# SSM input in scratch memory as it stands in its tile, and lag products with their sides exchanged, in a hybrid SSM and attention block

## The chip, the cores and the metric

The kernel runs on one NeuronCore of a Trainium2 chip. The metric is device time in microseconds (us); the time of a kernel is the median of its runs. Engines are named as in the profile: PE (TensorE), PEld (its weight loads), DVE (VectorE), ACT (ScalarE), POOL (GpSimd) and SP (SyncE, which issues most of the DMAs here). A q behind a name (SPq, POOLq) marks what an engine's sequencer issues.

## The reference

One layer over 2048 tokens of 1024 channels, in float32. In the core of it:

```
hn = rmsnorm(h, g_mix);  u, gate_ssm, q, k, v, gate_attn = split(hn @ w_in)     # 512 columns each
y_ssm = s5_branch(u, ...) * silu(gate_ssm)      # 32 groups of 16 channels, 64 complex states a group,
                                                # y = Re(C x) + D u, then GELU, then GLU
y_att = stick_breaking(q, k, v) * silu(gate_attn)                               # 8 heads of 64
h = h + concat(y_ssm, y_att) @ w_out
h = h + sigmoid(rmsnorm(h, g_ple) @ w_ple_gate) * (p @ w_ple_proj)
```

## The kernel before

The work has five stages. In the **u stage** (`phase_u`, `ssm_chain`) u = hn @ w_in[:, :512] is made for eight pairs of token tiles, T = 0 to 7, of 256 tokens each. In the **SSM stage** (`ssm_pack`, `ssm_batch`, `gate_unit`, the first `attn_proj`) eight batches of four groups go through the recurrence, while the gate of the SSM half and the first projections of attention are made. Then come the four passes of attention, into whose end the GLU is laid, and the two output products. Precise products are made of three float32r products (`mm3`): both sides are split into a high and a low part, the high one by ACT, the low one by DVE (`split`, L505).

**u stage.** For each T from 1 on, `load_x` loads two tiles x of 128 tokens, squares them with a sum on ACT (L599), makes the norm's factor r by a DVE operation (L498) and a power on POOL (L501), scales x by it on ACT (L604), transposes x on PE into `ps_x` (L605, the helper's line L520), splits the result into `xt` (L607, ACT L507 and DVE L66) and stores `xt` for later stages as `hn` (L608). T=0 is loaded transposed already (`load_plain`), and for T=0 and 1 (RAW = 2) the norm is not applied to x but to u, as a row `e.row[T]`, which `norms` makes (L577). Then 96 products of 256 columns a T fill four banks `ps_u` (L634, helper lines L535 to L537). ACT copies each bank to `uq` (L639), and for T < 2 POOL multiplies it by the row (L641). After T=3 and T=7 each of the four `uq` tiles, one for 128 channels, is stored by POOL (L644) to scratch `u` of shape [16, 128 channels, 128 chunks], in pieces of 64 values (256 B).

**The chain.** Beside it `ssm_chain` makes what depends on parameters alone: step sizes, exponentials and sines (small operations on DVE), powers of the decay for 16 steps (`cmul`, L221, on DVE), the factors fr and fis (L228 to L240), the scaled input matrices bb and bbs (L248 to L253, six operations of 128x512), and tables of rotations, whose products already lie on POOL (`cmul` with aside, L171 to L173), stored as `tb` (L300). `vt` (L65) is the helper for DVE operations of two operands; in a profile they carry its line, L66.

**SSM stage.** For each batch of four groups `ssm_pack` makes input matrices `bn` (DVE) and output matrices `stC` (POOL, L329 to L331), transposes `bn` on PE by fours into `ps_pack` (L337) and copies it to `stB` (ACT, L338). Then come the lag products (L343): eight float32 products with a 128x128 block of `bn` as the stationary side and 16 columns of `cts` as the moving side; their copy `lags` (L346) goes to memory, from which `raw` is loaded with shifts. `ssm_batch` loads `us` (L372), one transfer of 512 KB a batch in pieces of 2 KB, two buffers; it multiplies it by `stB` into `ps_b` (L391), rotates and scans on DVE, ACT and POOL, and after it makes the output in `ps_y` (L452 to L455), GELU and the store `z`. `gate_unit` makes 24 products for each of four `ps_sg` tiles a T (L659), in banks o and z0; ACT and DVE make the gate `sg`, stored as `gs` (L668).

**The order of the work.** The code does not fix it. A planner (`plan`, `list_schedule`, `best_order`, from L1304) knows a modelled duration of every instruction (`duration`, L1271) and schedules each engine's list greedily, by ranks that come from a pass backward in time, over six turns. Every engine, and each DMA queue, then runs its list in that order, and waits where an operand or a buffer is late. Hints bend the order: what stands under `e.first()` goes ahead of everything, a DMA under `e.later(T)` is not issued before the instruction behind `e.mark(T)` starts, what stands under `e.abreast()` stays together in its order. At T=2 (L626) the mark for the later weights is set: those of the gate and of the first attention pass, and late constants.

The diff and what calls it, with the line numbers that the profile uses:

Of the kernel before, what the change touches and what calls it, by code (L numbers as in the profile page):

```python
# [8 lines left out]
F32 = mybir.dt.float32  # L9
# [9 lines left out]
P = 128  # L19
# [32 lines left out]
RAW = 2  # L52
MARK0, MARK1 = 7, 6
# [122 lines left out]
def ssm_chain(e, keep, sm):  # L176
# [25 lines left out]
    bst, bsw, R.cts, R.ct2 = bs[:, 0], bs[:, 1], ct[:, 0], ct[:, 1]  # L202
    vs(nc, R.cts, R.cts, sgn, ALU.mult)
# [3 lines left out]
    vt(nc, x1, lr, dt, ALU.mult)  # L207
    small_exp(e, sm, mag, x1, G)
    vt(nc, th, li, dt, ALU.mult)
    small_sincos(e, sm, sn, cs, th, G)  # L210

# [92 lines left out]
def ssm_pack(e, sm, R, b):  # L304
# [29 lines left out]
    for q in range(GB * HS // 4):  # L334
        ps = e.bank("ps_pack", "w0", "w1")
        for k in range(4):
            nc.tensor.transpose(ps[:, k * P:(k + 1) * P], bnf[:, 4 * q + k], e.ident)  # L337
        nc.scalar.activation(mbf[:, 4 * q:4 * q + 4].rearrange("p g m -> p (g m)"), ps, AF.Copy)  # L338
    ps = e.bank("ps_pack", "w0", "w1")
    for s in range(HS):  # L340
        for k in range(GB):
            o = (s * GB + k) * GH
            nc.tensor.matmul(ps[:, o:o + GH], bnf[:, HS * k + s], R.cts[:, b * GB + k, :], start=True, stop=True)  # L343
# [17 lines left out]
def by_group(d, b):  # L361

    n = P // GH
    return d[b * GB // n].rearrange("(s j) (h g) c -> (j h) s (g c)", s=HS, h=GH)[:, :, b * GB % n * NCH:(b * GB % n + GB) * NCH]


def ssm_batch(e, pool, mb, mc, b):
# [4 lines left out]
    nc.sync.dma_start(us.rearrange("p s k c -> p s (k c)"), by_group(e.u_d, b))  # L372
# [167 lines left out]
def phase_u(e, pool, xp, chain):  # L540
# [50 lines left out]
    def load_x(T):  # L591
        xt = xp.tile([P, 2, 2, NC8, P], F32R, tag="xg", name="xt", bufs=2)
        for hf in range(2):
# [18 lines left out]
    with e.first():  # L612
        xts[0], w = load_plain(0)
        with e.later(0):
            xts[1] = load_x(1)
        norms()
    prep = chain()
    for T in range(NT // 2):
# [7 lines left out]
        if T == 2:  # L626
            e.mark(T)
# [8 lines left out]
        for ct in range(4):  # L636
            k0 = (T % 4) * n
            o, out = ps[ct].rearrange("p (c j) -> p j c", j=L), uq[ct][:, :, k0:k0 + n]
            nc.scalar.activation(out, o, AF.Copy)  # L639
            if T < RAW:  # L640
                nc.gpsimd.tensor_tensor(out, out, e.row[T].rearrange("p (c j) -> p j c", j=L), op=ALU.mult)  # L641
            if T % 4 == 3:
                c0 = (T // 4) * (NCH // 2)
                nc.gpsimd.dma_start(e.u_d[ct][:, :, c0:c0 + NCH // 2].rearrange("j p c -> p j c"), uq[ct])  # L644
# [3 lines left out]
def gate_unit(e, pool, w, T, xt):  # L648
# [6 lines left out]
    for ct in range(4):  # L655
        o = e.bank("ps_sg", "o", "z0")[:, :256]
# [382 lines left out]
def hybrid_block_kernel(ctx: ExitStack, tc: tile.TileContext, x, xt, small, p, w_in, ssm_w_glu, w_out, w_ple_gate,  # L1039
# [16 lines left out]
    e.u_d = [scratch(f"u{k}", [L, P, NCH]) for k in range(4)]  # L1056
# [82 lines left out]

    e.first, e.later, e.mark = (lambda: hint("first")), (lambda T=2: hint(T)), (lambda T: rows.append((len(nc.cur_bb.bb.instructions), T, "mark")))  # L1140
# [130 lines left out]
def duration(i, name, outs, ins, psum):  # L1271
# [5 lines left out]
    if name == "InstMatmult":  # L1277
# [6 lines left out]
        return (1 if half else 2) * max(cols / 1160.0, 0.056), 0.12  # L1284
# [220 lines left out]
def best_order(ops, pre, soft, length, mode, rows, turns=6):  # L1505

    first, last, inner, soon = set(), set(), set(), set()
    hints = [r for r in rows if len(r) == 3]
    mark = {T: a for a, T, kind in hints if kind == "mark"}
    for a, b, kind in hints:  # L1510
        for k in range(a, b):
            if kind == "first":
                soon.add(k)
            elif kind in mark and type(ops[k]).__name__ == "InstDMACopy":
# [14 lines left out]
    for _ in range(turns):  # L1529
        order, start, done = list_schedule(ops, pre, soft, length, mode, lead([k - 1e5 if k in soon else r for k, r in enumerate(rank)], first))  # L1530
# [67 lines left out]
```

## Time and profile before

| | |
|---|---|
| median of 3 runs | 1563.97 us (1562.64 to 1567.96) |
| the profiled execution | 1565.11 us, its span 1563.4 us |
| busy: PE, DVE, ACT, POOL | 1484.2, 1057.6, 931.2, 844.9 us |
| u stage (until the last copy of `ps_u`) | 0 to 131.6 us |
| SSM stage, roughly | 131.6 to 330 us |
| mean granted TensorE clock | 0.984 |

The profile shows one execution. Busy time is the time in which an engine had an instruction running; matmuls are pipelined, so that PE's busy time counts their overlap once, and the distance from one start to the next is what a product costs. An operation on a line is written as its output, an arrow and its inputs, by the names of the program's tiles. 128x512 f32 x16 means sixteen instructions on tiles of 128 partitions and 512 values. 64*128 after a PE instruction is the part of the array that it uses, rows by columns. A product of float32 operands appears as two instructions (passes). Text behind a group in brackets or bars says how long the engine had been idle before it, and who ended that.

### The profile page before, as it was taken

Reading aid. Unit: us, or ns where it says so; the run is one execution under the profiler, and the core shown is the slowest. Engines: PE = TensorE matmul, PEld = TensorE weight load, DVE = VectorE, ACT = ScalarE, POOL = GpSimd, SP = SyncE. Lnnn points to the kernel's source line nnn. Section 1 sums busy time; section 2 is a strip of 40 time slices with the busy share of each in tenths; the row PEclk is TensorE's granted clock in tenths of the full one; section 3 lists DMA queues with packets and bytes.
Section 4 is the critical chain, followed back from the end, with each engine's and each line's share of the span. In section 5 each row is a group of like instructions: output and inputs, shape, how many; then the busy total and the mean of one; then the engine's idle time right before and its main releaser. Section 6 shows DMA issues by size and latency. Waiting matters only on the chain.

```text
span 1563.4 us, 34915 instructions
## 1 busy us (share of the span) xinstructions
PE 1484.2 (95%) x13120; PEld 1261.9 (81%) x13120; DVE 1057.6 (68%) x1953; ACT 931.2 (60%) x2069; POOL 844.9 (54%) x1131
## 2 busy tenths in 40 slices
PE   8899999889999999998999988999999999999998
PEld 7899989878888888887888876777776888777776
DVE  7845868657677877678768785666869556754544
ACT  6553545456677877677867777666765435633432
POOL 3843433435556666565666598774565654433433
PEclk9999999999999999999999998999999999999999
DMA  8767636454332422334223365763347645622211
GB/s 334 273 248 216 205 109 208 147 182 157 139 110 95 134 94 95 108 116 136 91 89 116 127 222 167 234 181 95 104 147 252 200 162 182 196 68 93 89 61 61
DMA packets 168377, 236.22 MB, mean 151 GB/s; under 512 B 63504, under 2 KB 109712, under 8 KB 156816
## 3 DMA queue, kind: packets, MB, share of 16 engines
q1 hardware_dynamic: 166272, 226.50, 44.4%
q0 software_dynamic: 1936, 7.49, 1.7%
q8 instruction: 104, 1.70, 0.5%
q14 instruction: 65, 0.53, 0.1%
HBM read 169.05 MB, written 64.90 MB: 150 GB/s over the span
## 4 chain that ended last, share of the span: by engine, by line
PE 77%; DVE 8%; ACT 5%; issue 4%; POOL 3%; DMA 2%; POOLq 0%; SPq 0%; ACTq 0%; DVEq 0%
PE ps_q L744 20%; PE ps_o L848 6%; PE ps_z L809 6%; PE ps_wt L520 4%; PE ps_g L713 3%; PE ps_g L715 3%; PE ps_h L713 3%; PE ps_h L714 3%; PE ps_g L714 3%; PE ps_h L715 3%; DVE px L825 2%; DMA wst<-in_ssm_w_glu_dram 1%; PE ps_sg L535 1%; PE ps_u L535 1%; PE ps_u L536 1%
## 5 line engine op out<-in xcount | busy, mean ns | idle before, releaser
L827 POOL TENSOR_TENSOR be<-be,px 128x512 f32<-128x512 f32 (+3 forms) x320 | 317.3, 996 | 205.8 <-DVE px L825 157.2
L744 PE MATMUL ps_q<-w_w,xt 64*128 64x512 f32 x2880 | 406.1, 404 | 11.4 <-DVE v L66 9.7
L825 DVE TENSOR_TENSOR_SCAN px<-px,ps_z 128x512 f32<-128x512 f32 (+3 forms) x320 | 339.8, 1086 | 103.5 <-ACT be L819 73.8
L744 PEld LDWEIGHTS ps_q<-w_w,xt 64*128 64x128 f32 x2880 | 297.5, 187 | 52.8 <-issue 9.5
L814 ACT ACTIVATE px<-ps_z 128x512 f32<-128x512 f32 (+3 forms) x320 | 162.8, 540 | 76.9 <-PE ps_z L809 58.8
L840 ACT ACTIVATE ws<-ps_wt 128x512 f32<-128x512 f32 (+3 forms) x320 | 164.9, 550 | 62.7 <-PE ps_wt L520 62.4
L819 ACT ACTIVATE be<-ps_z 128x512 f32<-128x512 f32 (+3 forms) x320 | 167.8, 555 | 0.5 <-PE ps_wt L520 0.5
L809 PE MATMUL ps_z<-k,q 64*128 64x512 f32 (+3 forms) x960 | 148.9, 384 | 14.0 <-DVE px L825 11.1
L848 PE MATMUL ps_o<-ws,v 128*64 128x128 f32 x2176 | 140.1, 281 | 1.0 <-ACT ws L840 1.0
L848 PEld LDWEIGHTS ps_o<-ws,v 128*64 128x64 f32 x2176 | 120.3, 139 | 19.6 <-issue 15.6
L520 PEld LDWEIGHTS ps_wt<-ident,be 64*128 64x128 f32 x2176 | 104.5, 142 | 28.8 <-POOL be L827 8.9
L809 PEld LDWEIGHTS ps_z<-k,q 64*128 64x128 f32 x960 | 97.1, 189 | 33.3 <-DVE px L825 17.3
L520 PE MATMUL ps_wt<-ident,be 64*128 64x64 f32 x2176 | 111.5, 229 | 8.0 <-ACT ws L840 3.2
L1020 POOL TENSOR_TENSOR sg<-sg,h 128x512 f32<-128x512 f32 x32 | 44.8, 1411 | 114.3 <-DVE sg L66 114.3
L501 POOL TENSOR_TENSOR rs_qk<-rs_qk,mhalf 128x4 f32<-128x4 f32 x64 | 65.7, 1027 | 42.4 <-DVE rs_qk L73 41.6
L535 PE MATMUL ps_u<-xt,w_w 128*128 128x256 f32 x256 | 75.9, 297 | 6.6 <-ACT w_w L485 6.1
L536 PE MATMUL ps_u<-xt,w_w 128*128 128x256 f32 x256 | 75.4, 295 | 2.1 <-DVE xt L66 2.1
L66 DVE TENSOR_TENSOR yr<-sx,yr 128x512 fp32r<-128x512 f32 x64 | 53.4, 854 | 34.9 <-ACT yr L507 34.1
L823 POOL TENSOR_SCALAR_AFFINE_SELECT px<-px 128x128 f32<-128x128 f32 x128 | 39.4, 318 | 69.1 <-ACT px L814 67.5
L537 PE MATMUL ps_u<-xt,w_w 128*128 128x256 f32 x256 | 74.6, 294 | 0.0
L507 ACT ACTIVATE yr<-sx 128x512 fp32r<-128x512 f32 x64 | 39.3, 628 | 52.1 <-POOL sx L906 20.5
L1014 ACT ACTIVATE sg<-sg,rs 128x512 f32<-128x512 f32 x24 | 17.4, 725 | 74.0 <-DVE sg L66 74.0
(421 smaller groups left out, 3694.9 us busy)
## 6 DMA issues: line engine op xcount, KB each, us to landing
xt<-hn SPq DMA_DIRECT2D x60, 1024.0 KB, 4.9
hn<-xt SPq DMA_DIRECT2D x16, 1024.0 KB, 8.5
h<-h SPq DMA_DIRECT2D x64, 256.0 KB, 3.5
wst<-in_w_in_dram SPq DMA_DIRECT2D x48, 256.0 KB, 5.5
xg<-hn SPq DMA_DIRECT2D x12, 1024.0 KB, 7.0
out_dram<-sg SPq DMA_DIRECT2D x32, 256.0 KB, 2.5
x<-in_x_dram SPq DMA_DIRECT2D x14, 512.0 KB, 6.5
h<-in_x_dram SPq DMA_DIRECT2D x28, 256.0 KB, 4.4
```

Source lines behind the costliest of these rows:

```text
L520: e.nc.tensor.transpose(ps[h][:, 64 * k:64 * k + 64], v[r], e.ident[r, r])
L535: mm(out, wh, xh, start=first, stop=False)
L713: mm(out, xh, wh, start=first, stop=False, skip_group_check=more)
L714: mm(out, xh, wl, start=False, stop=False, skip_group_check=more)
L744: nc.tensor.matmul(o, xt[r, a, c], A.w[c][r, b], start=c + s == 0, stop=c == NC8 - 1 and s == 2)
L809: nc.tensor.matmul(z[:, :n], q[half[h], a], A.k[ch][half[h], b, :n], start=s == 0, stop=s == 2)
L814: nc.scalar.activation(px[:, :n], z[:, :n], AF.Sigmoid, scale=-(HD ** -0.5))
L819: nc.scalar.activation(be[:, :n], z[:, :n], AF.Sigmoid, scale=HD ** -0.5)
L825: nc.vector.tensor_tensor_scan(rv, rv, z[:, :n][:, ::-1], initial=1.0 if carry[h] is None else carry[h], op0=ALU.mult, op1=ALU.bypass)
L827: nc.gpsimd.tensor_tensor(be[:, :n], be[:, :n], px[:, 1:n + 1], op=ALU.mult)
L840: nc.scalar.activation(dst, ps, AF.Copy)
L848: nc.tensor.matmul(po[half[h], :P], A.v[sb][:, h], w[:, h, b], start=sb == i, stop=sb == 0)
```

## The change

The scratch `u` becomes eight arrays of [128 channels, 16, 64 chunks], one for each tile `uq`, so that a partition is stored as one piece of 4 KB, and SP issues the store instead of POOL. The load of `us` becomes sixteen transfers a batch of 32 KB each, in pieces of 64 values. The lag products exchange sides: four products a batch with 32 columns of `ct` as the stationary side and 256 columns of `bn` as the moving side, each on 32 columns of the array, put side by side in one bank; ACT copies them to `lt`, PE transposes that twice, and ACT copies the half that is wanted to `lags`.

With these come others. In `ssm_chain` the two-operand operations after the sines, and the power products, go from DVE to POOL. The row products of T=0 and 1 go from POOL to DVE; for T=1 DVE reads `ps_u` itself and ACT's copy is left out. `norms` is no longer under `e.first()`. The x transposes and their splits get a new hint, `ahead`, which lowers their rank by LEAD = 12 in the planner. The mark of the later weights goes from T=2 to T=4. `ps_pack` uses bank w0 alone, and `ps_sg` gets w1 as a third bank. The planner's duration of a float32 product on 32 columns or fewer becomes a quarter of that on the whole array.

```diff
+LEAD = 12
+LATER = 4
...
-    vt(nc, x1, lr, dt, ALU.mult)
+    nc.vector.tensor_tensor(x1, lr, dt, op=ALU.mult)
     small_exp(e, sm, mag, x1, G)
-    vt(nc, th, li, dt, ALU.mult)
+    nc.vector.tensor_tensor(th, li, dt, op=ALU.mult)
     small_sincos(e, sm, sn, cs, th, G)
+    def vt(nc, out, a, b, op):
+        nc.gpsimd.tensor_tensor(out, a, b, op=op)
...
-        cmul(e, sm, pr[:, n + 1:2 * n + 1], pi[:, n + 1:2 * n + 1], pr[:, 1:n + 1], pi[:, 1:n + 1], *bc, [n, G])
+        cmul(e, sm, pr[:, n + 1:2 * n + 1], pi[:, n + 1:2 * n + 1], pr[:, 1:n + 1], pi[:, 1:n + 1], *bc, [n, G], True)
...
     for q in range(GB * HS // 4):
-        ps = e.bank("ps_pack", "w0", "w1")
+        ps = e.bank("ps_pack", "w0")
...
-    ps = e.bank("ps_pack", "w0", "w1")
+    ps = e.bank("ps_pack", "w0")
+    flat = R.ct.rearrange("p k g h -> p (k g h)")
+    with e.abreast():
+        for k in range(GB):
+            o = (b * GB + k) * GH
+            nc.tensor.matmul(ps[2 * GH * k:2 * GH * (k + 1), :HS * P], flat[:, o:o + 2 * GH], bnf[:, HS * k:HS * (k + 1)].rearrange("p s m -> p (s m)"), start=True, stop=True)
+    lt = sm.tile([P, HS * P], F32, tag="lt", name="lt")
+    nc.scalar.activation(lt, ps[:, :HS * P], AF.Copy)
+    ps = e.bank("ps_pack", "w0")
     for s in range(HS):
-        for k in range(GB):
-            o = (s * GB + k) * GH
-            nc.tensor.matmul(ps[:, o:o + GH], bnf[:, HS * k + s], R.cts[:, b * GB + k, :], start=True, stop=True)
+        nc.tensor.transpose(ps[:, s * P:(s + 1) * P], lt[:, s * P:(s + 1) * P], e.ident)
...
-    nc.scalar.activation(lags[:, :HS], ps[:, :HS * GB * GH].rearrange("p (s g h) -> p s g h", s=HS, h=GH), AF.Copy)
+    nc.scalar.activation(lags[:, :HS], ps[:, :HS * P].rearrange("p (s g v h) -> p s g v h", s=HS, v=2, h=GH)[:, :, :, 0], AF.Copy)
...
-def by_group(d, b):
-    n = P // GH
-    return d[b * GB // n].rearrange("(s j) (h g) c -> (j h) s (g c)", s=HS, h=GH)[:, :, b * GB % n * NCH:(b * GB % n + GB) * NCH]
+def by_group(d, g, s):
+    return d.rearrange("(h g) (s j) c -> g s j h c", s=HS, h=GH)[g, s]
...
-    nc.sync.dma_start(us.rearrange("p s k c -> p s (k c)"), by_group(e.u_d, b))
+    half, n = NCH // 2, P // GH
+    for h in range(2):
+        for s in range(HS):
+            for k in range(GB):
+                g = b * GB + k
+                nc.sync.dma_start(us[:, s, k, h * half:(h + 1) * half], by_group(e.u_d[g // n][h], g % n, s))
...
-            for h, ps in enumerate(turned(e, "ps_x", ("tr", "ssm") if hf else ("z0", "z1"), [x[:, c * P:(c + 1) * P] for c in range(NC8)])):
-                d = slice(64 * h, 64 * h + 64)
-                split(e, xt[:, hf, 0, :, d], xt[:, hf, 1, :, d], ps)
+            with e.ahead():
+                for h, ps in enumerate(turned(e, "ps_x", ("tr", "ssm") if hf else ("z0", "z1"), [x[:, c * P:(c + 1) * P] for c in range(NC8)])):
+                    d = slice(64 * h, 64 * h + 64)
+                    split(e, xt[:, hf, 0, :, d], xt[:, hf, 1, :, d], ps)
...
     with e.first():
         xts[0], w = load_plain(0)
         with e.later(0):
             xts[1] = load_x(1)
-        norms()
+    norms()
...
-        if T == 2:
-            e.mark(T)
+        if T == LATER:
+            e.mark(2)
...
-            nc.scalar.activation(out, o, AF.Copy)
+            if T != 1:
+                nc.scalar.activation(out, o, AF.Copy)
             if T < RAW:
-                nc.gpsimd.tensor_tensor(out, out, e.row[T].rearrange("p (c j) -> p j c", j=L), op=ALU.mult)
+                vt(nc, out, o if T else out, e.row[T].rearrange("p (c j) -> p j c", j=L), ALU.mult)
             if T % 4 == 3:
-                c0 = (T // 4) * (NCH // 2)
-                nc.gpsimd.dma_start(e.u_d[ct][:, :, c0:c0 + NCH // 2].rearrange("j p c -> p j c"), uq[ct])
+                nc.sync.dma_start(e.u_d[ct][T // 4], uq[ct])
...
-        o = e.bank("ps_sg", "o", "z0")[:, :256]
+        o = e.bank("ps_sg", "o", "z0", "w1")[:, :256]
...
-    e.u_d = [scratch(f"u{k}", [L, P, NCH]) for k in range(4)]
+    e.u_d = [[scratch(f"u{k}{h}", [P, L, NCH // 2]) for h in range(2)] for k in range(4)]
...
-        return (1 if half else 2) * max(cols / 1160.0, 0.056), 0.12
+        return (0.5 if outs[0][0] <= 32 else 1 if half else 2) * max(cols / 1160.0, 0.056), 0.12
...
-        order, start, done = list_schedule(ops, pre, soft, length, mode, lead([k - 1e5 if k in soon else r for k, r in enumerate(rank)], first))
+        order, start, done = list_schedule(ops, pre, soft, length, mode, lead([k - 1e5 if k in soon else r - LEAD if k in ahead else r for k, r in enumerate(rank)], first))
```

More of the change, by code (lines that the diff above doesn't have):

```diff
@@ L202, in ssm_chain @@
     bst, bsw, R.cts, R.ct2 = bs[:, 0], bs[:, 1], ct[:, 0], ct[:, 1]
+    R.ct = ct
     vs(nc, R.cts, R.cts, sgn, ALU.mult)
@@ L1138, in hint @@
         rows.append((n, len(nc.cur_bb.bb.instructions), kind))
+    e.ahead = lambda: hint("ahead")
     e.first, e.later, e.mark = (lambda: hint("first")), (lambda T=2: hint(T)), (lambda T: rows.append((len(nc.cur_bb.bb.instructions), T, "mark")))
@@ L1505, in best_order @@
 def best_order(ops, pre, soft, length, mode, rows, turns=6):
-    first, last, inner, soon = set(), set(), set(), set()
+    first, last, inner, soon, ahead = set(), set(), set(), set(), set()
     hints = [r for r in rows if len(r) == 3]
@@ L1513, in best_order @@
                 soon.add(k)
+            elif kind == "ahead":
+                ahead.add(k)
             elif kind in mark and type(ops[k]).__name__ == "InstDMACopy":
```

## The prediction

> **What bounds the kernel now.** I read the page first, then the busy time by stage, then who waited for whom on PE, then the timeline around the longest waits. The page, and under it the u stage (0 to 131.6 us) and the SSM stage (to 330 us): after length and busy us of PE, weight loads, DVE, ACT and POOL, each row ends with PE's granted clock, DMA share and GB/s.
>
> ```profile
> span 1563.4 us, 34915 instructions
> PE 1484.2 (95%) x13120; PEld 1261.9 (81%) x13120; DVE 1057.6 (68%) x1953; ACT 931.2 (60%) x2069; POOL 844.9 (54%) x1131
> ...
> 0.00:131.60 131.60, 117.19 (x1049) 114.00 (x1050) 83.58 (x246) 69.74 (x128) 79.79 (x145) 0.96 0.75 270
> 131.60:330.00 198.40, 187.69 (x1473) 180.70 (x1472) 142.97 (x273) 96.44 (x219) 64.85 (x40) 0.98 0.56 174
> ```
>
> TensorE bounds both stages that the change touches: 187.69 of 198.4 us in the second. What the change is worth is therefore what it takes off PE's own work, and off PE's pauses. The pauses of the u stage, by who ended them (total us, times, longest), and three stretches of 8 us around them:
>
> ```profile
> PE ps_x L520 <- ACT x L604: 4.4, 2, 4.2
> PE ps_u L536 <- DVE xt L66: 2.1, 1, 2.1
> ...
> 20.00:28.00 8.00, 6.70 (x51) 6.29 (x50) 6.01 (x31) 6.79 (x16) 2.79 (x5) 0.79 1.02 421
> 40.00:48.00 8.00, 5.38 (x30) 5.18 (x31) 7.00 (x36) 3.99 (x7) 7.01 (x27) 0.79 0.90 295
> 74.00:82.00 8.00, 3.82 (x36) 3.57 (x31) 6.48 (x12) 3.21 (x5) 7.51 (x20) 0.79 1.05 309
> ```
>
> PE idles 1.30, 2.62 and 4.18 us there. Each time the granted clock averages 0.79 over the stretch, which loses another 8 x 0.21 = 1.7 us. So the three pauses cost 3.0, 4.3 and 5.9 us, 13.2 us together. The second waits for the splits on DVE, 7.00 of 8 us busy. The third is a chain through POOL, here in its order:
>
> ```profile
> 73.55 0.14 DVE L73 TENSOR_SCALAR rs_x<-ss 128x1 f32<-128x1 f32 x1
> 75.11 1.19 POOL L644 DMA_DIRECT2D u<-uq  x1
> 76.32 0.81 POOL L501 TENSOR_TENSOR rs_x<-rs_x,mhalf 128x1 f32<-128x1 f32 x1
> 77.17 1.15 ACT L604 ACTIVATE x<-x,rs_x 128x1024 f32<-128x1024 f32 x1 [4.04 <-POOL rs_x L501]
> ```
>
> The norm of the next x is ready at 73.69, but its power on POOL starts at 76.32, behind table products and the issue of a u store.
>
> **The change part by part.** *Moves between DVE, POOL and SP (u stage).* POOL loses the u stores and the row products; it gains most of the chain's two-operand work. Rows for the first two, then the prices of POOL products by size, then all engines from 40 to 90 us:
>
> ```profile
> L644 POOL DMA_DIRECT2D u<-uq x8 | 9.8, 1220 | 8.0 <-ACT uq L639 8.0
> L641 POOL TENSOR_TENSOR uq<-uq,row 128x256 f32<-128x256 f32 x8 | 6.9, 871 | 3.9 <-ACT row L575 2.7 <-ACT uq L639 1.1
> L173 POOL TENSOR_TENSOR tabs<-tabs,cp 128x32 f32<-128x32 f32 x4 | 1.2, 300 | 0.2
> L173 POOL TENSOR_TENSOR tabs<-tabs,cp 128x64 f32<-128x64 f32 x4 | 1.4, 362 | 0.1
> L173 POOL TENSOR_TENSOR tabs<-tabs,cp 128x128 f32<-128x128 f32 x4 | 2.4, 588 | 0.1
> L173 POOL TENSOR_TENSOR tabs<-tabs,cp 128x256 f32<-128x256 f32 x2 | 1.8, 904 | 0.0
> L403 POOL TENSOR_TENSOR swp<-swp,tabs 128x512 f32<-128x512 f32 x8 | 10.1, 1260 | 41.7 <-ACT swp L394 41.0 <-DVE gsq L77 0.7
> 40.00:90.00 50.00, 43.20 (x395) 41.88 (x396) 37.64 (x118) 27.02 (x48) 44.49 (x109) 0.93 0.81 285
> ```
>
> Added to POOL: four rounds of six power products, 6 x (0.300 + 0.362 + 0.588 + 0.904) = 12.9 us; six products of 512 for bb and bbs, 6 x 1.26 = 7.6; 21 products of 32, 6.3. That is 26.8 us against 9.8 + 6.9 = 16.7 removed. Between 40 and 90 us only four stores (4.9) and one row product (0.9) go, so POOL's 44.5 us of work become 65.5 us, 15.5 more than the 50 us hold. DVE loses the same 51 instructions and takes eight row products, at most the 0.87 us each that POOL took. Its splits, with the x transposes ahead of them, get a lead of 12 us in the planner's ranks. ACT loses four copies (T=1).
>
> So I expect the pauses at 20 and 40 us to go: the norms no longer push ahead of everything, and DVE is freed: 3.0 + 4.3 = **-7.3 us**. The third stays, because the power that it waits for is still on POOL, now with more in front of it, though the store at 75.11 is gone from its queue. Bounds: all three go, -13.2; or the 15.5 us of excess reach PE with one more clock loss, +17.2. I take the value between because POOL has room from 90 us on for what nobody awaits, and the planner, not the order of the code, decides who waits.
>
> *The later weights.* Their mark moves from T=2 to T=4.
>
> ```profile
> 43.36 1.39 SPq L480 DMA_DIRECT2D wst<-in_w_in_dram  x2
> ```
>
> T=3's last u store is issued at 75.11, so T=4 starts about there, and this first pair of gate weights moves behind it. Gate products begin after the u products, some 50 us later, which hides it: 0. Were that cover gone, PE would wait for a split, as it does once for 4.2 us above.
>
> *Lag products.* Rows: the 16 passes of one batch's lag products and the instruction after them; 16 full-width passes of 128 columns (L391) and their successor; 32 passes of 128 columns on half the array's columns (L848) and theirs; and x transposes between u products.
>
> ```profile
> 298.95 1.87 PE L343 MATMUL ps_pack<-cts,bn 128*128 128x16 f32 x16
> 300.67 0.36 PE L535 MATMUL ps_sg<-xg,w_w 128*128 128x256 f32 x1
> 301.11 1.95 PE L391 MATMUL ps_b<-us,stB 128*128 128x128 f32 x16
> 302.81 0.36 PE L535 MATMUL ps_sg<-xg,w_w 128*128 128x256 f32 x1
> ```
>
> ```profile
> 408.70 1.97 PE L848 MATMUL ps_o<-ws,v 128*64 128x128 f32 x32
> 410.60 0.73 PE L744 MATMUL ps_q<-w_w,xt 64*128 64x512 f32 x4
> ```
>
> ```profile
> 88.45 0.71 PE L520 MATMUL ps_x<-ident,x 64*128 64x64 f32 x16
> 89.09 0.39 PE L535 MATMUL ps_u<-xt,w_w 128*128 128x256 f32 x1
> 89.31 0.28 PE L536 MATMUL ps_u<-xt,w_w 128*128 128x256 f32 x1
> 89.43 0.28 PE L537 MATMUL ps_u<-xt,w_w 128*128 128x256 f32 x1
> ```
>
> Before, a batch takes 300.67 - 298.95 = 1.72 us, although each product moves only 16 columns: 0.11 us a pass, what a full-width pass of 128 columns takes (1.70 / 16 = 0.106). On half the columns a pass takes 1.90 / 32 = 0.059, so two run abreast. After, there are four products of 256 columns on 32 array columns each, 8 passes of 0.212: 1.70 us one behind the other, 0.85 two abreast, 0.42 four abreast. Two transposes add 0.21. The change of array shape costs about 0.1 us each way (the first u product after the transposes takes 0.22 us to its neighbour, the next 0.12), 0.2 in all. So 2.11, 1.26 or 0.83 us against 1.72; eight batches give +3.1, -3.7 or -7.1 us. Half the columns ran at half the price, so I take four abreast: **-7.1 us**. The extra copy of 128x256 lies on ACT, half idle in this stage (96.44 of 198.4). The pack's tiles now share one bank, a longer chain, which gate products cover.
>
> The Trainium skill ("TensorEngine Tiling (Array Packing)", Key Properties and Performance Considerations) promises up to 4x for 32 columns, but says that a change of tiling mode drains the array. The rows from 88.45 on show 0.1 us for it. With a full drain each way the gain would be smaller, toward the second rival.
>
> *The freed bank.* Gate tiles rotate over three banks instead of two.
>
> ```profile
> PE ps_sg L535 <- DVE sg L66: 2.7, 3, 1.5
> ```
>
> I count half of this wait, **-1.4** (bounds 0 and -2.7).
>
> *u through memory.* The store becomes pieces of 4 KB on SP, the load sixteen transfers of 32 KB in pieces of 256 B. Issues with median us to landing, the load's issue time, and the last load:
>
> ```profile
> u<-uq POOLq DMA_DIRECT2D x8, 512.0 KB, 6.9
> us<-u SPq DMA_DIRECT2D x8, 512.0 KB, 6.9
> lag<-lags SPq DMA_DIRECT2D x8, 96.0 KB, 2.0
> L372 SPq DMA_DIRECT2D us<-u x8: 360/370/516, 136.0 to 294.8; - x8
> 294.77 0.37 SPq L372 DMA_DIRECT2D us<-u  x1
> ```
>
> SP issues 16 x 0.37 = 5.9 us a batch, with lag, gate and z transfers queued behind it; gate products cover these. The last load has no cover: issued at 294.77, read at 301.11, 6.3 us. After, the last of sixteen is issued 5.9 us on and lands 2.0 us later or more (the 96 KB of lags), 6.9 at most (512 KB), so 1.6 to 6.5 us late; being the smaller transfer, it is nearer to the first: **+2.4**.
>
> Sum: -7.3 - 7.1 - 1.4 + 2.4 = -13.4. The profiled execution took 1565.11 us (span 1563.4), so 1551.7; it lies 1.1 above the median of the runs, so **1550.6 us**. Attention and output stages keep their operations; their order is planned anew, which I price at 0.
>
> **Rivals.**
> - All pauses go and the last load is hidden: 5.9 + 2.4 less, 1542.3. For it: the store leaves POOL, lead of 12 us. Against: POOL's 65.5 us.
> - One of the two savings fails. Lag products do not run abreast, or SSM's chain, not PE, sets the stage: 1550.6 + 7.1 = 1557.7. Or the two pauses reappear elsewhere: 1557.9. For it: DVE is 142.97 of 198.4 us busy and all reordered.
> - Both fail: about 1565.
> - Slower: POOL's queue between 40 and 90 us becomes the bound. Powers wait behind the moved products and PE waits 17.2 us more, pauses kept: 1550.6 + 7.3 + 17.2 = 1575.1. It decides once more than 6.1 + 4.7 = 10.8 of these us reach PE, 6.1 being what the other terms save and 4.7 what a measurement can tell. For it: POOL already made the longest pause. Against: it idles after 90 us.
> - Small pieces are slow. If 256 B halve a transfer's rate, the last load lands at 5.9 + 13.8 = 19.7 us, 13.4 late: 1561.6. Against: the old stores, in 256 B pieces too, landed in the same 6.9 us as loads of 2 KB. The Trainium skill ("DMA: Bandwidth & Descriptors", Specifications) states this rule, 512 B as the least for full rate; those two rows don't bear it out.
>
> **How the numbers follow.** Chances: forecast 0.34, all pauses 0.17, one saving fails 0.22, both fail 0.09, slow POOL 0.12, small pieces 0.06. A measurement tells apart about 0.3%, 4.7 us: under 1559.3 is faster, over 1568.7 slower. The first three cases give 0.73, less 0.05 for their edge; so faster 0.68, same 0.18, slower 0.14. The range, 1541 to 1567, spans the first four cases and small pieces; it leaves out slow POOL and little at the low end.
>
> **What would show it.** Right: no PE wait for xt splits before 60 us; the u stage ends some 7 us sooner; four lag products start within 0.1 us of each other and end in about 0.5 us; us loads in bursts of 6 us. Wrong: PE waits on ACT x L604 of more than 4.2 us (POOL), lag products 0.4 us apart, PE waiting for us at ps_b, or new PE pauses beyond 330 us.

## The result, and the profile after

The changed kernel takes **1579.35 us** (median of 4 runs, 1578.39 to 1582.76), the kernel before 1565.06 beside it (4 runs): ratio 1.0095, 95% interval [1.0069, 1.012]. It is 14 us slower where the prediction had it 13 us faster. The page of the profiled execution (1578.6 us), and under it the busy time by stretch, columns as before:

```profile
span 1576.9 us, 34955 instructions
PE 1485.3 (94%) x13072; PEld 1252.4 (79%) x13072; DVE 1044.2 (66%) x1910; ACT 933.3 (59%) x2073; POOL 852.6 (54%) x1166
```

```profile
0.00:131.60 131.60, 114.51 (x1023) 110.48 (x1024) 60.38 (x201) 67.05 (x123) 85.20 (x181) 0.96 0.71 268
129.40:340.40 211.00, 191.33 (x1470) 177.08 (x1468) 150.87 (x273) 101.98 (x230) 64.84 (x39) 0.98 0.56 168
20.00:28.00 8.00, 6.70 (x58) 6.09 (x54) 6.31 (x36) 7.31 (x15) 3.92 (x9) 0.79 1.01 420
40.00:48.00 8.00, 6.19 (x59) 5.92 (x58) 5.52 (x21) 3.37 (x6) 6.94 (x21) 0.94 0.38 128
40.00:90.00 50.00, 45.59 (x429) 43.84 (x428) 15.88 (x48) 26.02 (x47) 48.00 (x128) 0.97 0.69 251
74.00:82.00 8.00, 6.96 (x67) 6.48 (x65) 1.82 (x5) 4.57 (x9) 7.69 (x23) 1.00 1.03 371
```

The second row is the SSM stage. PE has 191.33 us of work in 211, so it idles 19.7 us, where it idled 10.7 of 198.4. The ends of the stages, read off the PE timeline as the starts of the last or first product of a kind (us):

| | last u product | last B product (`ps_b`) | last gate product | first attention product (`ps_q`) | span |
|---|---|---|---|---|---|
| before | 130.9 | 302.8 | 328.9 | 338.9 | 1563.4 |
| after | 129.3 | 316.5 | 340.3 | 351.6 | 1576.9 |

From the first `ps_q` to the end (span less its start) both take the same: 1224.5 and 1225.3 us. So nearly the whole loss lies ahead of it. By these ends the u stage gains 1.6 us and the SSM stage loses 13, but they do not cut the work at the same place: before, 36 gate products (4.5 us of PE) had run by the last u product, after, none. With these counted in the SSM stage, the u stage is some 3 us longer after, not shorter, and the SSM stage some 8. The last B product is 13.7 us late. These are PE's waits up to 342 us (total, times, longest):

```profile
PE ps_x L536 <- ACT x L620: 8.9, 6, 3.6
...
PE ps_b L407 <- DMA us<-u: 3.2, 3, 1.7
PE ps_y L471 <- DVE rot L68: 3.0, 2, 1.9
...
PE ps_sg L551 <- ACT w_w L501: 2.2, 2, 1.7
...
PE ps_sg L551 <- DVE sg L68: 0.5, 1, 0.5
```

The waits for `sg` that the freed bank was to shorten are 0.5 us now, 2.7 before. New are the waits for `us`; those for gate weights at `ps_sg` grow from 1.3 to 2.2. SP's instructions in front of the last batch, the issues of `us` as a group (min/median/max in ns), and PE at the last B products:

```profile
287.16 9.94 SPq L388 DMA_DIRECT2D us<-u  x16
297.20 0.87 SPq L477 DMA_DIRECT2D z<-gsq  x2
298.16 0.90 SPq L685 DMA_DIRECT2D gs<-sg  x2
299.15 0.45 SPq L390 DMA_DIRECT2D tabs<-tb  x1
299.69 0.87 SPq L671 DMA_DIRECT2D xg<-hn  x2
300.66 13.05 SPq L388 DMA_DIRECT2D us<-u  x16
```

```profile
L388 SPq DMA_DIRECT2D us<-u x128: 577/577/1361, 130.5 to 313.1; - x128
```

```profile
311.05 0.49 PE L407 MATMUL ps_b<-us,stB 128*128 128x128 f32 x2 [0.86 <-DMA us<-u]
311.29 0.36 PE L552 MATMUL ps_sg<-xg,w_w 128*128 128x256 f32 x1
311.50 0.28 PE L553 MATMUL ps_sg<-xg,w_w 128*128 128x256 f32 x1
313.52 3.32 PE L407 MATMUL ps_b<-us,stB 128*128 128x128 f32 x14 [1.75 <-DMA us<-u]
```

An issue takes 0.577 us, not 0.37, and the sixteen of each of the last two batches 9.9 and 13 us. The last burst stands behind the one before it, and PE twice waits for `us` at the last B products. The lag products, by contrast, came out as predicted; here are one batch's four (two passes each) and its transposes:

```profile
133.81 0.64 PE L350 MATMUL ps_pack<-bn,cts 128*32 128x256 f32 x8
134.38 0.38 PE L552 MATMUL ps_sg<-xt,w_w 128*128 128x256 f32 x1
134.60 0.28 PE L553 MATMUL ps_sg<-xt,w_w 128*128 128x256 f32 x1
...
134.96 0.43 PE L355 MATMUL ps_pack<-ident,lt 128*128 128x128 f32 x2
135.15 0.36 PE L553 MATMUL ps_sg<-xt,w_w 128*128 128x256 f32 x1
```

Eight passes take 134.38 - 133.81 = 0.57 us, four abreast; with the transposes' 0.19 it is some 0.8 us in place of 1.72. PE's busy time on `ps_pack` falls from 25.7 to 18.5 us ahead of attention. PE saved its 7 us there, and the kernel did not: PE's busy time as a whole is even 1.1 us longer.

### The profile page after: what moved, and what is told of

Same layout as the page of the kernel before. It is cut to its first block, busy times and chain, and to the rows that moved or that the text cites. A ratio compares the mean times of both kernels' runs of the same rounds, so it can differ in the third digit from the quotient of the medians.

```text
span 1576.9 us, 34955 instructions
## 1 busy us (share of the span) xinstructions
PE 1485.3 (94%) x13072; PEld 1252.4 (79%) x13072; DVE 1044.2 (66%) x1910; ACT 933.3 (59%) x2073; POOL 852.6 (54%) x1166
## 5 line engine op out<-in xcount | busy, mean ns | idle before, releaser
L826 PE MATMUL ps_z<-k,q 64*128 64x512 f32 (+3 forms) x960 | 150.3, 387 | 13.8 <-DVE px L842 10.7
L79 DVE SCALAR_TENSOR_TENSOR w_w<-wst,gmix,w_w 128x512 fp32r<-128x512 f32 x48 | 45.2, 952 | 24.8 <-ACT w_w L501 24.2
```

The costliest lines, as they stand in the source:

```text
L826: nc.tensor.matmul(z[:, :n], q[half[h], a], A.k[ch][half[h], b, :n], start=s == 0, stop=s == 2)
```

## The experiments

Two theories were to be told apart. **Theory**: the SSM stage is set by the chain of its eight batches (load, B product, rotation and scan, y product), not by PE's work; the change slows this chain by sixteen issues a batch on SP and by the chain's products on POOL. **Rivals**: small pieces are slow to land; the buffers, the planner's order or the later mark make the loads late. All runs (us, each beside the kernel before on the same chip, which took 1565.2 to 1566.9):

| kernel | median | ratio to before, 95% |
|---|---|---|
| changed, u through memory as before | 1562.7 | 0.9978 [0.9963, 0.9992] |
| before, with the new layout of u alone | 1574.4 | 1.0042 [1.0023, 1.0061] |
| before, with the new lag products alone | 1565.7 | 0.9993 [0.9976, 1.0009] |
| changed, chain on DVE | 1570.3 | 1.0021 [1.0006, 1.0036] |
| before, four loads of 256 B pieces | 1562.1 | 0.9973 [0.9958, 0.9987] |
| before, eight loads of 256 B pieces | 1566.3 | 1.0001 [0.9988, 1.0014] |
| before, sixteen loads of 512 B pieces | 1582.8 | 1.0110 [1.0084, 1.0135] |
| before, two of three gate products | 1555.9 | 0.9934 [0.9911, 0.9956] |
| **changed, u as before and chain on DVE** | **1546.3** | **0.9877 [0.9851, 0.9904]** |
| that, with the old lag products | 1556.1 | 0.9938 [0.9918, 0.9959] |
| that, with the early mark | 1546.7 | 0.9882 [0.9867, 0.9897] |
| that, with spare loads on SP | 1563.0 | 0.9973 [0.9956, 0.9990] |
| changed, three buffers for us | 1580.7 | 1.0093 [1.0067, 1.0120] |
| changed, early mark | 1568.9 | 1.0023 [1.0007, 1.0039] |
| changed, true issue cost in the planner | 1578.1 | 1.0084 [1.0056, 1.0113] |
| changed, half the loads on ACT | 1583.0 | 1.0116 [1.0101, 1.0131] |
| before, later mark alone | 1564.1 | 0.9990 [0.9974, 1.0005] |

**One part undone or done alone.** First the layout of u taken back out of the changed kernel, then put alone into the kernel before:

```diff
-                nc.sync.dma_start(us[:, s, k, h * half:(h + 1) * half], by_group(e.u_d[g // n][h], g % n, s))
+    nc.sync.dma_start(us.rearrange("p s k c -> p s (k c)"), by_group(e.u_d, b))
...
```

> The kernel after, with the scratch u, its pieces of 256 B in the store and the one load of 512 KB a batch as before; the store stays on SP. Theory (the sixteen loads, by their issue of about 0.6 us each on SP or by their small pieces, stretch the SSM stage): that stage, 211 us after and 198 before, falls to about 191, since the lag products save 7; time about 1559. Rival (late gate weights): the gate weights still start at T=4, so about 1575. Rival (more products on POOL): u stage and rest unchanged, about 1577.

> The kernel before with the new scratch u alone: stores of 4 KB pieces on SP, sixteen loads a batch. Theory (loads): slower by 13 to 20 us, 1578 to 1585, with SP busy some 10 us a batch with them. Rivals (late weights, POOL): the loads are hidden, 1562 to 1567.

Undone, it gives 1579.4 - 1562.7 = 16.6 us (1562.7 where the theory expected about 1559); the SSM stage comes down to 197.5 us, not to 191. Done alone, it costs 8.2, less than the 13 to 20 expected: this run also takes the store of u off POOL, so 8.2 is not the price of the loads alone. Next the lag products alone (the matmul, copy and transposes of the diff, in the kernel before):

> The kernel before with the exchanged lag products alone (the pack's tiles still rotate over two banks; the planner knows their new duration). If PE's work bounds the SSM stage: 7 us faster, about 1558. If the longer chain of copies and transposes takes it back: 1563 to 1566.

Nothing is gained. Its SSM stage, from the last u product on, beside the same row of the kernel before (198.00 us, PE busy 188.10):

```profile
126.10:331.20 205.10, 188.19 (x1467) 176.68 (x1465) 148.21 (x273) 99.61 (x227) 71.60 (x44) 0.97 0.58 176
```

The last u product starts 4.8 us earlier, but only because the 36 gate products now run behind it; the last gate product is later (331.2, before 328.9). PE idles 16.9 us in this stage in place of 9.9: what it saves becomes idle time. This run alone cannot tell whether the batches hold PE up in any case or whether the longer chain of copies and transposes does it; the same exchange gains 9.8 us in another version below, so that chain does not take it back everywhere. Then the chain's products on DVE again, in the changed kernel:

```diff
-    def vt(nc, out, a, b, op):
-        nc.gpsimd.tensor_tensor(out, a, b, op=op)
...
-        cmul(e, sm, pr[:, n + 1:2 * n + 1], pi[:, n + 1:2 * n + 1], pr[:, 1:n + 1], pi[:, 1:n + 1], *bc, [n, G], True)
+        cmul(e, sm, pr[:, n + 1:2 * n + 1], pi[:, n + 1:2 * n + 1], pr[:, 1:n + 1], pi[:, 1:n + 1], *bc, [n, G])
```

> The kernel after with the chain's products back on DVE. Theory (the loss is in the SSM stage, by the loads): within 4 us of the kernel after, 1575 to 1582. Rival (the products on POOL delay the powers and with them x): the waits of PE for the scaling of x, 8.9 us after, go, and it is 5 to 9 us faster, 1570 to 1574.

The theory's 1575 to 1582 missed, and the rival came: POOL costs 9.1 us there. The last u product starts at 123.1 in place of 129.3 (no gate product ahead of it in either), and PE's waits for the scaling of x fall from 8.9 to 4.1 us.

**What bounds the SSM stage.** PE's work is cut by 30 us, with no other edit (the planner orders the rest anew):

```diff
-            mm3(e, o, (w[c][:, 0, cs], w[c][:, 1, cs]), (xt[:, :, 0, c], xt[:, :, 1, c]), c == 0, c == NC8 - 1)
+            nc.tensor.matmul(o, w[c][:, 0, cs], xt[:, :, 0, c], start=c == 0, stop=False)
+            nc.tensor.matmul(o, w[c][:, 0, cs], xt[:, :, 1, c], start=False, stop=c == NC8 - 1)
```

> The kernel before without one of the three products of every gate tile (low part of the weight by high part of x), so the gate is less exact: 256 products fewer, at 0.119 us each some 30 us less work for PE in the SSM stage, and nothing else changed. If PE's own work sets the stage: 25 to 31 us faster, 1535 to 1541. If the chain of the batches sets it (loads, rotation on DVE, B and y products): 0 to 10 us faster, PE's idle time in the stage grows by the rest of the 30, and the last B product ends within 8 us of where it ended before (302.8).

9.7 us come out of 30. The row of its SSM stage:

```profile
129.10:318.20 189.10, 166.24 (x1238) 158.62 (x1237) 141.31 (x271) 96.56 (x219) 70.54 (x42) 0.93 0.61 188
```

PE now idles 22.9 us in place of 9.9, the granted clock falls from 0.98 to 0.93, and the last B product starts at 299.1 (302.8 before). Of the 20 us that do not come out, 13 are idle time of PE, and some 7 went into slower products, as PE's busy time in the stage falls by 21.9 us where the products left out should have made it 29. So a third of PE's work still counted, at the upper edge of what the second branch allowed, but for the larger part the batches set this stage; a PE that is 95% busy was filling their gaps with gate products.

**Why sixteen loads cost.** Size of pieces or count: the kernel before with four, eight and sixteen loads a batch. The diff is that of four; for eight, each is split in two by `k`; for sixteen, by `k` and by halves of the partitions, with whole rows of 512 B.

```diff
-    nc.sync.dma_start(us.rearrange("p s k c -> p s (k c)"), by_group(e.u_d, b))
...
+    for h in range(2):
+        for s in range(HS):
+            nc.sync.dma_start(us[:, s, :, h * half:(h + 1) * half], src[s][:, b * GB % n:b * GB % n + GB, h * half:(h + 1) * half])
```

> The kernel before, with each batch's u loaded by four transfers of 128 KB in pieces of 256 B, in place of one of 512 KB in pieces of 2 KB. If the number of issues on SP is what delays the batches: four issues of 0.4 to 0.6 us put the last one 1.2 to 1.8 us behind the first, and the time stays within 3 us of before (1563 to 1569 where before takes 1566). If the small pieces are what is slow (rival): the layout alone cost 8 us with the same 256 B, so about 1574, and PE waits for us at ps_b as long (7 us in seven places).

> The kernel before with eight loads of us a batch, 64 KB each in pieces of 256 B. Between four (1562.1) and sixteen (1574 to 1583). If SP's time is the cost and it grows with each issue of some 0.6 to 0.8 us: 5 to 6 us a batch, 1565 to 1571. If only a threshold matters, so that eight still hide behind gate products: 1560 to 1566.

> The kernel before, with each batch's u loaded by sixteen transfers of 32 KB in pieces of 512 B, on 64 partitions each. Count theory: sixteen issues on SP, the last 9 us behind the first as in the changed kernel; PE waits for us at ps_b by 5 us or more, and the time is 1571 to 1578 (the layout alone gave 1574). Rival, small pieces: pieces of twice the size take away most of the 8 us, so 1566 to 1569. If an issue takes 0.37 us here and not 0.58, the bursts are 6 us and the time falls between, 1569 to 1571.

The issue groups of the three, in this order, with the landing of the first and the last (KB each, median us from issue to landing):

```profile
L376 SPq DMA_DIRECT2D us<-u x32: 359/505/3451, 139.5 to 299.8; - x32
```

```profile
us<-u SPq DMA_DIRECT2D x32, 128.0 KB, 4.6
```

```profile
L377 SPq DMA_DIRECT2D us<-u x64: 360/467/2997, 135.0 to 296.8; - x64
```

```profile
L377 SPq DMA_DIRECT2D us<-u x128: 444/594/1944, 135.9 to 323.4; - x128
```

```profile
us<-u SPq DMA_DIRECT2D x128, 32.0 KB, 2.2
```

The pieces are not the cause: 256 B in four or eight loads cost nothing, 512 B in sixteen cost 17 us, more than the 5 to 12 expected. Nor do small transfers land slowly, 2.2 us. What goes with the cost is the count: four loads are 3.5 us faster than one, eight equal it, sixteen are 8 to 17 us slower. The result for eight (1566.3) lies in the range of a cost that grows with each issue and just above that of a threshold, so it does not choose between them. Nor do the runs say why the two versions of sixteen differ by 8.4 us: the form of the loads differs, and so does the engine that stores u (SP at 1574.4, POOL at 1582.8).

The Trainium skill ("DMA: Bandwidth & Descriptors", Anatomy of one DMA) says of transfers issued by GpSimd that the fixed cost lies in completion and that setup is small. That is about the time of one transfer; what counts in these rows is how long an issue holds the queue of SP, 0.59 us each with sixteen loads. The Trainium skill's section Bandwidth on the same page, measured on transfers issued by GpSimd, gives 64 KB as the size below which descriptors dominate a transfer. The costly sixteen of 32 KB lie below it and the harmless eight of 64 KB on it, so the rule points the right way, although 32 KB land in 2.2 us here.

Next, three buffers for `us` in place of two, and a planner that knows the price:

```diff
-    us = pool.tile([P, HS, GB, NCH], F32, tag="us", bufs=SSM_DEPTH, name="us")
+    us = pool.tile([P, HS, GB, NCH], F32, tag="us", bufs=3, name="us")
...
-        return (0.6 if eng == "Pool" else 0.45), 0.0
+        return (0.6 if eng == "Pool" else 0.62 if outs[0][1] == NCH // 2 else 0.45), 0.0
```

> The changed kernel (1579) with three buffers for us in place of two, so that a batch's sixteen loads no longer wait for the y products of the batch two before. If the loads are late because they start late (buffer) and then take 10 us of issues: the loads move ahead, PE's 3.2 us of waits for us go, the last B product ends near 303 to 308, and the time falls to 1565 to 1571. If it is the time of SP that is missing whenever they are issued (what else SP issues stands behind them): 1576 to 1581, with ACT's waits for gate weights unchanged.

> The changed kernel with the planner told 0.62 us for each of the sixteen issues in place of 0.45, nothing else changed but the order that it then plans. If the loss is the order (the planner puts products and other transfers where the loads cannot yet have landed): 5 to 12 us faster, 1567 to 1574. If the loss is the issues themselves: within 4 us of the changed kernel, 1575 to 1583.

Both stay within 1.4 us of the changed kernel. With the true price in the planner PE no longer waits for `us` at `ps_b` at all, and the time stays; so those waits of PE are not what the loads cost. The third buffer does not bring the loads forward; the last one goes out at 314.4 us, not 313.1:

```profile
L388 SPq DMA_DIRECT2D us<-u x128: 577/577/1438, 132.4 to 314.4; - x128
```

Then another issuer:

```diff
-                nc.sync.dma_start(us[:, s, k, h * half:(h + 1) * half], by_group(e.u_d[g // n][h], g % n, s))
+                (nc.scalar if k % 2 else nc.sync).dma_start(us[:, s, k, h * half:(h + 1) * half], by_group(e.u_d[g // n][h], g % n, s))
```

> The changed kernel with eight of each batch's sixteen loads issued by ACT in place of SP. If it is SP's queue that is missing (about 80 us of loads in a stage in which it also issues gate, z, lag and weight transfers): SP gets 38 us back, ACT, half idle, takes them, and the time falls by 6 to 14 us, 1565 to 1573. If many small transfers are slow to land, whoever issues them (rival): 1576 to 1582. If ACT has no room for 38 us more: over 1582, with PE waiting for ACT at ps_b, ps_y or ps_sg.

1583.0 lies on the edge of the second and third branch (the runs go from 1581.7 to 1585.6); ACT's timeline speaks for the third: its own work stands still while it issues. PE does wait for ACT, though at `ps_pack` (14.6 us for `lt` and `lags`, 2.4 in the changed kernel) and not where I had named it. ACT's waits in that stage, put down to the issues, follow the timeline:

```profile
135.40 1.39 ACTq L388 DMA_DIRECT2D us<-u  x1
...
136.81 3.30 ACTq L388 DMA_DIRECT2D us<-u  x5
140.16 0.28 ACT L358 ACTIVATE lags<-ps_pack 128x128 f32<-128x128 f32 x1 [3.86 <-DMA us<-u]
```

```profile
ACT tp L462 <- DMA us<-u: 13.3, 4, 4.6
...
ACT lt L352 <- DMA us<-u: 10.3, 2, 8.2
```

So an issue of this form costs either engine 0.58 us (medians: SP 0.577 in the changed kernel, ACT 0.586 here), and ACT is on the batches' chain too. Last, does SP's time hurt through u itself, or through what else waits in that queue? Sixteen spare loads a batch, into a tile that nothing reads, in the version without the two costs:

```diff
     nc.sync.dma_start(us.rearrange("p s k c -> p s (k c)"), by_group(e.u_d, b))
...
+                nc.sync.dma_start(spare[:, s, k, h * half:(h + 1) * half], src[s][:, b * GB % n + k, h * half:(h + 1) * half])
```

> The version that took 1546.3, with sixteen spare transfers a batch added on SP: 32 KB each in pieces of 256 B, into a tile that nothing reads. So SP issues as much as in the changed kernel, and DMA moves 4 MB more, but u itself still comes by one transfer that nothing splits. If the loads cost because SP's time is taken from the other transfers of the stage (gate weights, gate and z stores, lags): 1555 to 1570, with ACT's waits for wst or raw back at 7 us or more. If they cost because u itself is complete only 10 us after its first issue, while the batches wait: 1545 to 1550.

They cost 16.7 us by the medians, 15 by the ratios, at 0.43 us an issue, while u itself was on time (PE waits 0.4 us for it). The issues, and what ACT waits for now:

```profile
L388 SPq DMA_DIRECT2D spare<-u x128: 319/431/3208, 131.4 to 270.6; - x128
```

```profile
ACT sg L683 <- DMA gs<-sg: 12.7, 4, 5.6
...
ACT tp L462 <- DMA raw<-lag: 6.0, 4, 3.0
```

A gate tile's buffer comes free only when its store has gone out, and the lags are loaded late; without the spare loads ACT waits 2.0 us for the gate stores and not at all for the lags. (I had named `wst` or `raw` as what would wait; mostly it was the gate stores.) With sixteen loads of u itself the same version takes 1570.3, 7.3 more, so the larger part of the cost seems to fall on the neighbours in the queue, the smaller on u. Not shown is how much of the 16.7 is SP's time and how much the 4 MB that the spare loads move besides.

**The two costs apart and together.** Both edits (u as before, chain on DVE) in the changed kernel:

> The changed kernel with u through memory as before (one load a batch, pieces of 2 KB) and the products of the chain back on DVE. If the two costs are separate and add: the loads were worth 16.6 us (1579.4 to 1562.7) and the chain on POOL 9 us (1579.4 to 1570.3), so 1579.4 - 16.6 - 9 = about 1554, with the u stage ending near 123 us and the SSM stage 198 us after it. If the two hide each other (rival: POOL's lateness only mattered because the batches were late): 1560 to 1563, no better than with the chain on POOL.

**1546.3 us**, 19 faster than before and below the 1554 of the sum: the costs more than add. u as before gives 16.6 with the chain on POOL and 24.0 with it on DVE; the chain 9.1 and 16.4. Its two stages:

```profile
0.00:127.00 127.00, 114.64 (x1036) 110.55 (x1037) 72.57 (x252) 66.22 (x122) 66.81 (x130) 0.99 0.79 274
127.00:313.80 186.80, 179.12 (x1438) 168.31 (x1437) 148.68 (x274) 100.51 (x229) 66.13 (x39) 1.00 0.62 189
```

PE idles 7.7 us in the SSM stage, at full granted clock. What POOL delays shows beside the version with the chain on POOL (u as before in both). First with the chain on POOL: PE's waits for x, the loads of `us`, the last products of the rotation tables and the loads of the tables (first and last start in us behind the durations):

```profile
PE ps_x L532 <- ACT x L616: 9.1, 8, 3.2
```

```profile
L384 SPq DMA_DIRECT2D us<-u x8: 359/398/1182, 139.6 to 293.3; - x8
L175 POOL TENSOR_TENSOR tabs<-tabs,cp x14: 259/365/891, 69.2 to 99.0; 128x32 f32<-128x32 f32 x4, 128x64 f32<-128x64 f32 x4, 128x128 f32<-128x128 f32 x4, 128x256 f32<-128x256 f32 x2
L386 SPq DMA_DIRECT2D tabs<-tb x8: 320/326/424, 138.7 to 287.5; - x8
```

Then with the chain on DVE:

```profile
PE ps_x L529 <- ACT x L613: 4.0, 5, 1.7
```

```profile
L381 SPq DMA_DIRECT2D us<-u x8: 370/375/952, 129.7 to 275.6; - x8
L175 POOL TENSOR_TENSOR tabs<-tabs,cp x14: 270/492/1068, 48.9 to 82.7; 128x32 f32<-128x32 f32 x4, 128x64 f32<-128x64 f32 x4, 128x128 f32<-128x128 f32 x4, 128x256 f32<-128x256 f32 x2
```

The tables are ready 16 us earlier, but with the chain on POOL they were ready at 99.0 and first loaded at 138.7, so nothing shows that a batch waited for them. What the rows do show is x: PE waits 5 us less for it, the last u product starts at 127.0 in place of 133.9, the first load of `us` 9.9 us earlier, and the first B product at 136.0 in place of 145.4. At the last B product the lead has grown from 9.4 to 17.6 us (288.9, 306.5). So about half of the delay enters with u itself, for the most part by way of x; where the batches lose the rest is open.

Do PE's savings pay here? The lag products go back to 16 passes:

```diff
-            nc.tensor.matmul(ps[2 * GH * k:2 * GH * (k + 1), :HS * P], flat[:, o:o + 2 * GH], bnf[:, HS * k:HS * (k + 1)].rearrange("p s m -> p (s m)"), start=True, stop=True)
...
+            nc.tensor.matmul(ps[:, o:o + GH], bnf[:, HS * k + s], R.cts[:, b * GB + k, :], start=True, stop=True)
```

> The version that took 1546.3 (u as before, chain on DVE), with the lag products as they were: 16 passes of 1.72 us a batch in place of four abreast. If the batches no longer hold PE up there, PE's 7.1 us come back in full: 1552 to 1555. If PE's work does not set the stage there either, as it did not when the lag products alone were changed (1565.7 against 1566.2): 1545 to 1549.

They do: 9.8 us by the medians, 6.5 by the spans of the profiles (1551.5 and 1545.0), around the 7.1 worked out. Here PE's work counts, in a stage in which it idles only 7.7 us.

**The later mark.** LATER = 2 in the changed kernel, the same in the best version, and the late mark alone in the kernel before:

> The changed kernel with the mark of the later weights back at the u stage's third tile (LATER = 2). By the prediction it costs and saves nothing: 1576 to 1582. If the later mark delays the gate weights so that the batches or the first gate products start late (rival): 3 to 8 us faster, and ACT waits less for wst than the 11.9 us of the changed kernel.

> The version that took 1546.3 (u as before, chain on DVE) with the mark of the later weights at the third tile. If the later mark costs 10 us by itself, as between the changed kernel and its version with the early mark (1579 to 1569): 1536 to 1541. If it cost that only where SP's queue was full of loads, so that the weights came late: 1544 to 1549.

> The kernel before with the mark of the later weights moved to the fifth tile, nothing else. By the prediction 0: 1563 to 1568. If the mark delays the gate weights by itself: 1570 to 1577, with ACT or DVE waiting for wst and the first gate products later than 124.0.

10.4 us in the changed kernel, nothing in the other two. In the changed kernel ACT waits for the gate weights, also behind bursts of loads on SP:

```profile
ACT w_w L501 <- DMA wst<-in_w_in_dram: 11.9, 6, 6.4
```

In its early-mark version this wait is gone from the list, and the first gate product starts at 122.8, not 129.8. Such a wait of ACT is not a cost by itself: with eight loads a batch in the kernel before it is 11.5 us, and the time 1566.3. That the late mark costs only where SP's queue is full fits all three runs; but each edit also makes the planner order everything anew, and the order could not be kept fixed. This holds for every comparison here: it is of an edit and of the order that the planner then finds.

## Why the prediction was wrong

- **What bounds the kernel.** "What the change is worth is therefore what it takes off PE's own work" failed for the SSM stage. PE was busy 187.69 of 198.4 us, and still 30 us less work gave 9.7. The rival "SSM's chain, not PE, sets the stage" came closer, and it was priced only as a lost saving, not as a place where new delays on that chain lengthen the stage: the changed kernel's last B product is 13.7 us late, with PE idle 19.7 us.
- **u through memory** (+2.4, 1.6 to 6.5) is the step that failed most: taken out of the changed kernel it is worth 16.6 us with the chain on POOL, 24.0 with it on DVE. The issue took 0.58 us, not 0.37, a figure from a transfer of other shape. Worse was the clause "gate products cover these" for what is queued behind: the spare loads, u itself on time, cost 16.7 us. The trace of before held the warning, eight batches in 200 us with nearly every store and load of the stage on one queue; 128 x 0.37 = 47 us more in it should have been a rival of its own.
- **POOL.** The rival "slow POOL" had one of the two causes, 15.5 us too much work between 40 and 90 us (POOL is busy 48.00 of these 50); that its 1575.1 lies near the measured time is luck, as it counted neither the loads nor what they cost. PE's pauses at 40 and 74 us shrank (idle 1.81 and 1.04 us in these stretches, before 2.62 and 4.18; granted clock 0.94 and 1.00, before 0.79), the first stayed, and six waits for `x`, 8.9 us, stand in place of two, 4.4. With the later start of the batches that follows it is worth 9.1 to 16.4 us.
- **Pauses of the u stage** (-7.3): the size came near, the places did not, so in part this is luck. The version with the old lag products and both costs out is 9.8 us faster than before, where this term and the freed bank make -8.7. Its three stretches:

```profile
20.00:28.00 8.00, 6.70 (x55) 6.10 (x52) 6.48 (x40) 7.11 (x15) 3.03 (x6) 0.79 1.01 421
40.00:48.00 8.00, 7.13 (x70) 6.86 (x69) 6.44 (x29) 3.37 (x6) 6.32 (x26) 1.00 0.51 172
74.00:82.00 8.00, 6.38 (x64) 6.11 (x62) 3.15 (x6) 3.66 (x6) 7.54 (x16) 1.00 0.97 268
```

  The pause at 20 us, forecast to go, is as it was: the product into `ps_row` waits about 1 us for a split on DVE, before, after and here. The one at 40 us mostly went, and so did the one at 74 us, which was forecast to stay. The last u product starts 9.0 us earlier (121.9), but half of that is the 36 gate products, 4.5 us, that now run behind it. The sum also charged the lower clock to PE's idle time: on its busy time the loss is 1.4 and 1.1 us at the first two pauses, not 1.7 each.
- **Lag products** (-7.1): mechanism and size right, four abreast, 0.8 us a batch; the changes of shape stayed inside the 0.57 us and the next product's 0.22. The Trainium skill ("TensorEngine Tiling (Array Packing)", Theoretical Speedup) promises up to 4x for a dimension of 32 or less; the 0.57 us, against 1.70 worked out for one behind the other, agree with the direction and make a factor of 3 with the change of shape. The savings paid in the version without the two costs, not in the kernel before.
- **The later weights** (0): right alone and in the best version, wrong by up to 10.4 us in the changed kernel, the case for which I had named the cover and not asked whether it would last. Nor do gate products begin only after the u products, as I wrote: before, the first starts at 124.0.
- **Small pieces**: the trace's verdict against this rival held, with 256 B in four and eight loads.
- **The rest of the kernel** (0): from the first `ps_q` on it held within 1 us.

The savings of the sum without its loads, -7.3 - 7.1 - 1.4 = -15.8, stand against -19.3 measured in the version that keeps them and drops the two costs. The costs were put at +2.4 and measure 33.1 (1579.4 - 1546.3). Still open: how the costs share between the late x, the batches and the late weights, since they hide and raise each other; how SP's time and the added traffic share in the spare loads; and the 3.5 us that four loads gained, for which no run gives a cause.

## What to carry to other kernels

A busy share near 95% did not make PE the bound here, because it had work that can fill any gap: take some of that work away and see whether the stage shrinks. Count a queue's issues as work of that queue, with the price of the new shape, and ask for everything behind them who waits for it. And move work to an idle engine only if it is idle at that time, and if what it then delivers late has slack.

## What the runs showed of the hardware

- The issue of a transfer cost SP 0.37 us (median) for 512 KB in pieces of 2 KB, 0.47 for 64 KB and 0.51 for 128 KB in pieces of 256 B, and 0.43 to 0.59 for 32 KB in the forms tried here; single ones took up to 3.5. On ACT (0.59) it stops ACT's arithmetic: behind five issues in 3.30 us an operation had waited 3.86.
- 32 KB in pieces of 512 B landed 2.2 us after their issue, 128 KB in pieces of 256 B after 4.6.
- Four float32 products of 256 columns on 32 array columns each took 0.57 us for all eight passes, from the first to the start of the next full-width product.
- The mean granted clock was lower in most stages with more idle time of PE, but not in order: 1.00 in an SSM stage with 7.7 us idle, 0.96 to 0.98 with 10 to 20, 0.93 with 22.9, and 0.97 with 26.1 (half the loads on ACT).
